# A gated delta-rule kernel on one core: inverses and their coupling moved into the tile of A, five k/q buffers, earlier loads for the next head's inverses

## The chip, the cores and the metric

The kernel runs on one core of one Trainium2 chip. The metric is device time in microseconds (us) for one execution of the whole program; the time of before is the median of 3 runs. Engines are named as the profile names them: PE (matmul), PEld (its weight loads), DVE, ACT, POOL and SP (which issues all DMAs of this kernel, in program order). PEq, SPq and so on are the sequencers.

## The reference

One layer with two parallel branches over 2048 tokens of width 1024, fed by one input projection to 7 x 1024 columns. Group A is a gated MLP with spatial mixing over blocks of 128 tokens. Group B, which the change is about, is a gated DeltaNet with 8 heads of width 128, in chunks of 64 tokens:

```
A  = strict_lower((k*beta) @ k.T * L)            # 64 x 64, L = decay between positions
T  = inverse(I + A)                              # triangular
u  = T @ (v*beta);  w = T @ (k*beta*exp(decay))
v_new = u - w @ state
o     = (q*exp(decay)) @ state + (q @ k.T * L) @ v_new
state = state*exp(decay_last) + (k*exp(decay_last - decay)).T @ v_new
```

Then a normalisation and a gate for the branch, the output projection, a gated per-layer embedding and a last normalisation. The state runs through all 32 chunks of a head, so those steps follow one another; everything else is a large projection.

## The kernel before, in words

The tokens go in two passes of 1024, and in each pass the 8 heads follow one another. In a pass PE first computes the v columns of group A (`v_unit`), then for each head three units of projections: `kq_unit` (k and q), `vu_unit` (v of group B, u of group A) and `zz_unit` (two gates). A unit is 2 column blocks x 2 token blocks (b = 0, 1) of 512 tokens, 24 products `pj` each, in three-product float32r splits (high and low parts). The weights of a unit come by four DMAs (`raw`, L251) and are split by ACT and DVE into `whi` and `wlo`. After the heads follow `out_stream` (`pso`) and `gate_stream` (`pe`, `pg`).

Beside this stream runs the work of group B, for each head in four stages. Two chunks (128 tokens, index u of 4, in each b) share one 128 x 128 tile:

- `front` (L719): transposes k, forms `pkq` = k'[k q] on PE, and from it the tiles `AT` (A, transposed and scaled) and `QK`; the two diagonal 64 x 64 blocks of each AT go to DRAM (`atd`, L780).
- `inverse` (L811): POOL solves the 16 systems of a head at once by 63 steps of two tensor_tensor each (L179: multiply to `xtmp`, subtract from `xs`). The systems come back from DRAM in eight pieces `ain` (L822, two buffers), the unit matrix in `xs` (L815). The inverses are stored to `td` (L841) and loaded into the two diagonal blocks of the one tile `Dt` (L848), but only after the outputs of the head before are finished (`done`, L844).
- `chain` (L851): for each of 8 tiles u in turn seven float32 products of 128 columns: k with the state (`pc<-S,kq`), Dt with r (`pc<-r,Dt`, in the very first tile of a head of the first pass `pc<-vn,Dt`), q with the state (`po<-S,kq`), AT with the first half of that result (`pc<-x,AT`), Dt with the corrected r, then kd with w (the new state) and QK with w (the output).
- `finish` (L919): normalises, transposes and gates the output and stores it (`done`).

The order of every engine's instructions is fixed when the program is built. The class `Flow` (L31) plays a clock: `mm` advances it on PE, `fl.op` books the other engines (`gtt`, L178, books a POOL tensor_tensor at 330 + 1.6 ns for each element), tasks sleep until a given time (`yield fl.t + 4500`), and `drive` and `step` put a task's instructions into PE's stream of projections when the clock says that its data are there. What the clock says is not what the chip does: on the chip each engine goes through its list in order and waits at semaphores. So an instruction whose data come later than the clock said holds up all that stands behind it on its engine. `take`, `give` and `free` with the table CAPS (L103) keep count of buffers: four `kq` tiles are two heads.

Of the kernel before, what the change touches and what calls it, by code (L numbers as in the profile page):

```python
# [18 lines left out]
ALU = mybir.AluOpType  # L19
# [83 lines left out]
CAPS = {"pj": 2, "tr": 2, "m": 2, "kq": 4, "pre": 2, "acc": 3, "uz": 3, "ot": 1, "gn": 2, "R": 2, "raw": 4, "w": 5}  # L103
# [3 lines left out]
def trunk(tc, a, out):  # L107
# [78 lines left out]
    with ExitStack() as outer:  # L186
# [18 lines left out]
        bsd = [dp.tile([P, P], F32, name=f"bsd{i}") for i in range(NH)]  # L205
        hsc = [dp.tile([P, D], F32, name=f"hsc{i}") for i in range(NT)]
# [82 lines left out]
        def x_load(row0, halves=False):  # L289
            xs = []  # L290
            for i in range(4):
# [5 lines left out]
                else:  # L297
                    xt = [gt("kq", "xt", [P, D], 4)]
# [54 lines left out]
        def inv_rms(xs):  # L353

            dg = gt("xs", "dg", [P, 4, P], 1)
# [16 lines left out]
        def prep_store(p):  # L372
            for b in range(2):
# [5 lines left out]
                for i in range(4):  # L379
                    xs.append([gt("kq", "xt", [P, D], 4)])  # L380
                    dma(xs[i][0], a["x"][row0 + i * P:row0 + (i + 1) * P, :])
                    yield fl.t + 1500
# [47 lines left out]
        def scalars(ab):  # L430
            beta = gt("beta", "beta", [P, 64], 2)
            act(beta, ab[:, 8:16].rearrange("p f t -> p (f t)"), AF.Sigmoid)
            yield fl.t + 3500
            yield from fl.take("gn")
# [27 lines left out]
            pc = bank("tr", "pcs", [P, 3, 64])  # L462
            for i, m in enumerate((uincl, mgt, ones)):
                g0 = mm(pc[:, i, :], m, g, True, True)
            ex = gt("ex", "ex", [P, 3, 64], 2)
# [173 lines left out]
        def zz_unit(X, p, ui, h, st, norms, mids):  # L639
# [14 lines left out]
            for b in range(2):  # L654
                yield lambda: len(done) >= st["i"] + b - 3
                ps = yield from proj(X, ui, 0, b)
                fl.spawn(z_silu(ps, st), 170, 1)
                if b == 0:
                    next_w(ui + 1, 0)
            if mids:  # L660
                banks = yield from proj_both(X, ui, 1, mids)
            for b in range(2):
                ps = banks[b] if mids else (yield from proj(X, ui, 1, b, rest_w(ui + 1) if b else None))
                fl.spawn(z_post(ps, st["U"], b, gz), 170, 1)
            fl.spawn(mix(p, h, gz, ws, bs, gns, norms), 1500, 2)

        def kq_unit(X, p, ui, h, st):
# [3 lines left out]
            for b in range(2):  # L671
                yield fl.free("kq")
                fl.used["kq"] = fl.used.get("kq", 0) + 1
                kq = gt("kq", "kq", [P, 4, 2, P], 4)
# [44 lines left out]
        def front(p, h, b, st):  # L719
            beta, gh, gl, ex, ne = SC[p]  # L720
            cs = slice(h * 8 + b * 4, h * 8 + b * 4 + 4)
            while len(done) < st["i"] + b - 3 or len(fronts) < st["i"] + b:
# [7 lines left out]
            qe = gt("qe", "qe", [P, 4], 4)  # L730
# [14 lines left out]
            tt(bn, bn, beta[:, cs], ALU.mult)  # L745
            st["iv"][b] = power(iv, iv, phalf[:, :4], after=f)
            AT = gt("AT", "AT", [P, 4, P], 4)
            QK = gt("QK", "QK", [P, 4, P], 4)
            for u2 in range(2):
# [24 lines left out]
                fl.give("m")  # L774
            yield f
# [7 lines left out]
            st["B"].append((kq, kd, vn, AT, QK, bn, qe))  # L783
# [27 lines left out]
        def inverse(p, h, st):  # L811
            while 2 * len(inverted) < st["i"]:
                yield fl.t + 300
            xs = gt("xs", "xs", [P, 8, 64], 1)
            dma(xs, a["xinit"])  # L815
            tmp = gt("xtmp", "xtmp", [P, 160], 1)
# [23 lines left out]
            td = dp.tile([64, 16, 64], F32, tag="td", bufs=2, name="td")  # L840
            dma(td.rearrange("(k c) s i -> (c s) k i", c=8), xs)  # L841
            inverted.append(1)
            yield fl.t + 2600
            while len(done) < st["i"]:  # L844
                yield fl.t + 300
# [536 lines left out]
```

## Time and profile before

| | |
|---|---|
| median of 3 runs | 2336.96 us (2334.66 to 2454.31) |
| the profiled execution | 2334.43 us, span 2332.7 us from the first to the last instruction |
| granted PE clock, mean over the span | 0.985 of full speed |
| busy: PE, PEld, DVE, ACT, POOL | 96%, 81%, 55%, 43%, 49% of the span |

The stages can be read from the timeline by tile names: the first pass's heads run from about 125 to 907 us, those of the second from about 996 to 1720 us, then the output projection to 2085 us and the gate to the end. A granted clock of 1.00 is 2.4 GHz, 0.50 is 1.2 GHz. Busy times of PE are modelled ends of a pipeline; the distance between the starts of two products tells what one costs in a dense stretch.

### The profile page before, as it was taken

To read this page: it belongs to the slowest core of one execution; us is meant where nothing else is said; L and a number is where in the kernel's file an instruction comes from. 1 tells how busy PE (TensorE), PEld (TensorE's weight loads), DVE (VectorE), ACT (ScalarE), POOL (GpSimd) and SP (SyncE) were. 2 spreads that over 40 slices of the span, in tenths; PEclk is the share of its full clock that TensorE was granted. 3 is DMA by queue.
4 is the path that set the end of the run, shared out by engine and by line. 5 is a ranking of instruction groups with operands and counts; after the bars stand their busy time and mean duration, and the time that the engine had idled before them with its cause. 6 is when DMAs were issued, how large, how long until landed. Compare 5 with 4: busy or idle time off the path is not lost.

```text
span 2332.7 us, 34766 instructions
## 1 busy us (share of the span) xinstructions
PE 2250.4 (96%) x11884; PEld 1878.9 (81%) x11884; DVE 1293.3 (55%) x2845; ACT 999.1 (43%) x2398; POOL 1131.6 (49%) x2246
## 2 busy tenths in 40 slices
PE   8999899999999999999899999999989999999998
PEld 8988688787787779987788878778778878878886
DVE  5465375574665755347466566575664243346665
ACT  5554354453444443445345454454432232244443
POOL 1118668586686772137768668668660000001111
PEclk9999999999999999999999999999999999999999
DMA  5632232323222243222332332232453466452221
GB/s 185 228 117 88 73 99 79 98 72 101 89 87 80 79 148 114 77 76 80 89 98 80 96 99 78 87 87 85 126 167 121 150 200 194 139 185 74 79 77 63
DMA packets 249201, 253.22 MB, mean 109 GB/s; under 512 B 66112, under 2 KB 163904, under 8 KB 249024
## 3 DMA queue, kind: packets, MB, share of 16 engines
q1 hardware_dynamic: 249024, 251.01, 34.6%
q8 instruction: 93, 1.52, 0.3%
q14 instruction: 84, 0.69, 0.1%
HBM read 195.89 MB, written 55.05 MB: 108 GB/s over the span
## 4 chain that ended last, share of the span: by engine, by line
PE 78%; POOL 11%; DMA 5%; issue 2%; DVE 2%; ACT 1%; SPq 1%; POOLq 0%; DVEq 0%; ACTq 0%
PE pj L121 36%; PE pso L121 13%; PE pg L121 7%; PE pc L121 6%; PE pv L121 6%; POOL xs L179 5%; POOL xtmp L179 4%; DMA Dt<-td 2%; PE po L121 2%; PE pe L121 2%; PE pkq L121 1%; DMA wo<-in_wo 1%; DMA td<-xs 1%; PE pm L121 1%; PE ph L127 1%
## 5 line engine op out<-in xcount | busy, mean ns | idle before, releaser
L179 POOL TENSOR_TENSOR xtmp<-ain,xs 128x132 f32<-128x132 f32 (+47 forms) x1008 | 462.4, 459 | 250.9 <-DMA ain<-atd 180.4
L179 POOL TENSOR_TENSOR xs<-xs,xtmp 128x132 f32<-128x132 f32 (+47 forms) x1008 | 483.2, 479 | 79.0
L175 POOL TENSOR_TENSOR rstd<-rstd,nhalf 128x1 f32<-128x1 f32 x64 | 45.8, 722 | 577.3 <-DVE rstd L159 290.3
L121 PE MATMUL pj<-xlo,whi 128*128 128x512 f32 x768 | 315.3, 411 | 0.0
L121 PE MATMUL pj<-xhi,wlo 128*128 128x512 f32 x768 | 314.9, 410 | 0.0
L121 PE MATMUL pj<-xhi,whi 128*128 128x512 f32 x768 | 314.2, 409 | 0.0
L121 PE MATMUL pj<-xrhi,whi 128*128 128x512 f32 x768 | 313.2, 408 | 0.0
L121 PE MATMUL pj<-xrhi,wlo 128*128 128x512 f32 x768 | 312.3, 407 | 0.0
L121 PE MATMUL pj<-xrlo,whi 128*128 128x512 f32 x768 | 311.0, 405 | 0.0
L152 DVE SCALAR_TENSOR_TENSOR acc<-pre,cw,acc 128x512 f32<-128x512 f32 x288 | 227.8, 791 | 23.9 <-ACT acc L135 19.4
L121 PE MATMUL pso<-wolo,yhi 128*128 128x512 f32 x512 | 204.9, 400 | 2.3 <-DVE wolo L148 2.2
L121 PE MATMUL pso<-wohi,ylo 128*128 128x512 f32 x512 | 205.3, 401 | 0.0
L121 PE MATMUL pso<-wohi,yhi 128*128 128x512 f32 x512 | 202.5, 395 | 0.0
L148 DVE TENSOR_TENSOR wlo<-raw,whi 128x512 fp32r<-128x512 f32 x224 | 163.9, 734 | 62.5 <-ACT whi L135 61.6
L135 ACT ACTIVATE whi<-raw 128x512 fp32r<-128x512 f32 x224 | 140.3, 629 | 95.2 <-PE pj L121 71.0
L135 ACT ACTIVATE yhi<-yraw 128x512 fp32r<-128x512 f32 x128 | 80.3, 630 | 215.3 <-PE pso L121 208.6
L121 PEld LDWEIGHTS pj<-xlo,whi 128*128 128x128 f32 x768 | 147.2, 192 | 24.3
L121 PEld LDWEIGHTS pj<-xhi,wlo 128*128 128x128 f32 x768 | 147.0, 191 | 23.9
L121 PEld LDWEIGHTS pj<-xhi,whi 128*128 128x128 f32 x768 | 146.9, 191 | 23.7
L121 PEld LDWEIGHTS pj<-xrhi,wlo 128*128 128x128 f32 x768 | 145.7, 190 | 25.1
L121 PEld LDWEIGHTS pj<-xrlo,whi 128*128 128x128 f32 x768 | 146.0, 190 | 24.5
L148 DVE TENSOR_TENSOR ylo<-yraw,yhi 128x512 fp32r<-128x512 f32 x128 | 89.5, 701 | 135.9 <-ACT yhi L135 133.2
(202 smaller groups left out, 4858.3 us busy)
## 6 DMA issues: line engine op xcount, KB each, us to landing
raw<-in_wu SPq DMA_DIRECT2D x224, 256.0 KB
ain<-atd SPq DMA_DIRECT2D x128, 256.0 KB
yraw<-ysc SPq DMA_DIRECT2D x128, 256.0 KB
vsc<-gv SPq DMA_DIRECT2D x64, 128.0 KB
gn<-vsc SPq DMA_DIRECT2D x32, 256.0 KB
ysc<-gn SPq DMA_DIRECT2D x32, 256.0 KB
ysc<-zb SPq DMA_DIRECT2D x32, 256.0 KB
wo<-in_wo SPq DMA_DIRECT2D x32, 256.0 KB
```

The source lines that it names most:

```text
L121: nc.tensor.matmul(o, lhsT, rhs, start=start, stop=stop)
L127: nc.tensor.transpose(o, i, ident)
L135: nc.scalar.activation(o, i, func, **kw)
L148: nc.vector.tensor_tensor(o, x, y, op)
L152: nc.vector.scalar_tensor_tensor(o, x, sc, y, op0, op1)
L175: nc.gpsimd.tensor_tensor(o, x, y, ALU.pow)
L179: nc.gpsimd.tensor_tensor(o, x, y, op)
```

## The change

The inverses no longer go to a tile of their own. They are loaded into the diagonal blocks of the tile `AT` itself, from which A's diagonal has been stored before. The lower left block of that tile holds the coupling of the two chunks (rescaled by ACT with a new decay factor `ex[:, 3]`), and a new task `join` computes the block above the diagonal: the coupling already multiplied by an inverse, four products of 64 columns for each b (`pgt`) and one DVE multiplication. A tile u of the chain is then six products instead of seven, four of which depend on one another (k with the state, M with r0, M with r, kd with w). Also changed: the inverses may be loaded before the head before is finished; the next head's unit matrix (`xs`, now two buffers) and first piece `ain` are loaded when 56 of the 63 steps are done (`solved`), and the POOL loop follows 1000 ns on the planner's clock after the loads instead of 4500; `front` waits for the chain two heads back (`chained`), not for its finished output; `kq` has five buffers; `gtt` is booked at 375 + 1.95 ns; the two halves of `zz_unit` are exchanged; the state between the passes is kept in DRAM (`ssc`) and loaded at the head of the chain (`S0`); two masks come in one late load. The diff, cut to its core:

```
-CAPS = {... "kq": 4, ...}
+CAPS = {... "kq": 5, ...}
 def gtt(o, x, y, op, after=None):
-        return fl.op("pool", 330 + 1.6 * width(o), after)
+        return fl.op("pool", 375 + 1.95 * width(o), after)
 def front(p, h, b, st):
-            while len(done) < st["i"] + b - 3 or len(fronts) < st["i"] + b:
+            while len(chained) < st["i"] + b - 3 or len(fronts) < st["i"] + b:
...
+            tt(fb, bn, ex[:, 3, cs], ALU.mult)
...
-                    stt(AT[:, u], pkq[:, j, 0], bn[:, u:u + 1], L[:, u], ALU.mult, ALU.mult)
+                    f = stt(AT[:, u], pkq[:, j, 0], bn[:, u:u + 1], L[:, u], ALU.mult, ALU.mult)
+                    act(AT[64:128, u, 0:64], pkq[64:128, j, 0, 0:64], AF.Copy, after=f,
+                        scale=ex[64:128, 3, h * 8 + b * 4 + u:h * 8 + b * 4 + u + 1])
...
+            nc.vector.memset(AT[0:64, :, 64:128], 0.0)
 def inverse(p, h, st):
+            while 2 * len(solved) < st["i"]:
+                yield fl.t + 300
+            xs = gt("xs", "xs", [P, 8, 64], 2)
+            dma(xs, a["xinit"])
             load(0)
+            while 2 * len(inverted) < st["i"]:
+                yield fl.t + 300
             load(1)
-            yield fl.t + 4500
+            yield fl.t + (1000 if h else 4500)
...
-                if jj == 7 and jc < 6:
+                if jj == 7:
                     yield f
-                    load(jc + 2)
+                    if jc < 6:
+                        load(jc + 2)
+                    else:
+                        solved.append(1)
...
             yield fl.t + 2600
-            while len(done) < st["i"]:
-                yield fl.t + 300
-            for d in range(2):
-                dd = slice(d * 64, d * 64 + 64)
-                dma(Dt[dd, :, dd], td.rearrange("c (u d) i -> d c u i", d=2)[d])
-            fl.spawn(chain(p, h, st), 4500, 0)
+            for b in range(2):
+                for d in range(2):
+                    dd = slice(d * 64, d * 64 + 64)
+                    dma(st["B"][b][3][dd, :, dd], td[:, b, :, d])
+            fl.spawn(join(0, st), 5000, 0)
+            fl.spawn(join(1, st), 5600, 1)
+            fl.spawn(chain(p, h, st), 5000, 0)
+def join(b, st):
+            M, fb = st["B"][b][3], st["B"][b][6]
+            yield from fl.take("tr")
+            pg = bank("tr", "pgt", [P, 4, 64])
+            for u in range(4):
+                f = mm(pg[:, u], M[:, u], M[:, u, 64:128], True, True)
+            yield f
+            f = tt(M[0:64, :, 64:128], pg[0:64], fb[0:64, :, None].to_broadcast([64, 4, 64]), ALU.mult)
+            fl.give("tr")
+            yield f
+            st["G"].append(b)
 def chain(p, h, st):
-            while len(done) < st["i"] or len(st["R"]) < 2:
+            while len(chained) < st["i"] or len(st["R"]) < 2:
                 yield fl.t + 300
-            Sp = state[:, h, :]
+            if p:
+                Sp = gt("S0", "S0", [P, P], 1)
+                dma(Sp, ssc[h])
...
-                        yield stt(r, pc[:, 0], ne[:, cu], vn[:, u], ALU.mult, ALU.add)
-                    f = mm(pc[:, 1], Dt[:, b * 4 + u], r, True, True)
+                        f = stt(r0[lo], pc[lo, 0], ne[lo, cu], vn[lo, u], ALU.mult, ALU.add)
+                        stt(r[up], pc[up, 0], ne[up, cu], vn[up, u], ALU.mult, ALU.add)
+                    yield f
+                    f = mm(pc[:, 1], M[:, u], r0, True, True)
...
-                    yield act(x1[0:64], pc[0:64, 1], AF.Copy)
-                    f = mm(pc[:, 2], AT[:, u], x1, True, True)
+                    f = act(r[lo], pc[lo, 1], AF.Copy, scale=-1.0)
+                    act(w[lo], pc[lo, 1], AF.Copy, scale=bn[lo, uu])
+                    yield f
+                    f = mm(pc[:, 2], M[:, u], r, True, True)
...
-                    yield tt(r[64:128], r[64:128], pc[64:128, 2], ALU.subtract)
-                    yield mm(pc[:, 1], Dt[:, b * 4 + u], r, True, True)
-                    yield ts(w, pc[:, 1], bn[:, u:u + 1], None, ALU.mult)
+                    yield ts(w[up], pc[up, 2], bn[up, uu], None, ALU.mult)
...
+                        if last:
+                            dma(ssc[h], Sn)
...
+                chained.append(1)
```

How this moves instructions is read from the order of the built programs. On PE, at the start of the chain of head 2 of the first pass, this stands in before (`pkq` is the front of head 3, `pj` the projections, `pq` transposes of q):

```order
L121 MATMUL pkq<-kqlo,kqhi 128x256
L121 MATMUL pkq<-kqhi,kqlo 128x256
L121 MATMUL pj<-xhi,whi 128x512
L121 MATMUL pc<-vn,Dt 128x128
L121 MATMUL pj<-xlo,whi 128x512
L121 MATMUL pj<-xhi,wlo 128x512
L121 MATMUL pj<-xhi,whi 128x512
L121 MATMUL pc<-x_218,AT 128x128
L121 MATMUL pj<-xlo,whi 128x512
```

And this in the changed kernel, at the start of the same chain:

```order
L121 MATMUL pj<-xhi,wlo 128x512
L121 MATMUL pj<-xhi,whi 128x512
L121 MATMUL pgt<-AT 128x64 x8
L121 MATMUL pc<-r_220,AT 128x128
L121 MATMUL pj<-xlo,whi 128x512
L121 MATMUL pj<-xhi,wlo 128x512
L121 MATMUL pj<-xhi,whi 128x512
L121 MATMUL pc<-r,AT 128x128
L121 MATMUL pj<-xlo,whi 128x512
```

The front of head 3 is gone from there: its last `pkq` stood one `pj` ahead of the chain and now stands 70 `pj` ahead of it. Head 2's own last `pkq` lies 288 `pj` ahead of its chain in before, and 349 now. Eight joins stand at the chain's start.

On SP, around the store (`td`) and the load (`Dt`) of head 1's inverses in the first pass, before (`atd` is head 2's front, `ain` its systems; `ws`, `bs`, `raw` and `gn` are loads for the projection units and the mixing):

```order
L780 DMA atd_3726<-AT_3566 64x4x64 x2
L841 DMA td_3758<-xs_2883 128x8x64
L848 DMA Dt_217<-td_3758 64x8x64 x2
L780 DMA atd_3726<-AT_3785 64x4x64 x2
L815 DMA xs_3901<-in_xinit 128x512
L822 DMA ain_3904<-atd_3726 128x1x512
L822 DMA ain_3906<-atd_3726 128x1x512
L642 DMA ws_4012<-in_ws 128x128
L645 DMA bs_4015<-in_bs 128x128
L251 DMA raw_4017<-in_wu 128x512
```

The same place in the changed kernel, where the inverses are loaded into the tiles AT:

```order
L831 DMA ain_3953<-atd_3735 128x1x512
L649 DMA ws_4004<-in_ws 128x128
L652 DMA bs_4007<-in_bs 128x128
L252 DMA raw_4009<-in_wu 128x512
L252 DMA raw_4011<-in_wu 128x512
L252 DMA raw_4013<-in_wu 128x512
L252 DMA raw_4015<-in_wu 128x512
L659 DMA gn_4017<-vsc0_73 128x4x128
L659 DMA gn_4019<-vsc0_73 128x4x128
L860 DMA td_4029<-xs_2931 128x8x64
L831 DMA ain_4031<-atd_3735 128x1x512
L866 DMA AT_2588<-td_4029 64x4x64 x2
```

The first piece of the next head's systems is loaded ahead of the store of the inverses, and eight loads of the projections and the mixing now stand between the two; in before these stood behind the load of the inverses.

On SP in the second pass, in the changed kernel, the load of the state `S0` for head 6's chain stands behind loads of the output stage (`wo`, `yraw`) and of the mixing (`gn`):

```order
L1012 DMA wo_18504<-in_wo 128x512
L1059 DMA yraw_18507<-ysc0_75 128x4x128
L1059 DMA yraw_18509<-ysc0_75 128x4x128
L1059 DMA yraw_18511<-ysc0_75 128x4x128
L1059 DMA yraw_18513<-ysc0_75 128x4x128
L659 DMA gn_18518<-vsc1_74 128x4x128
L659 DMA gn_18520<-vsc1_74 128x4x128
L1059 DMA yraw_18529<-ysc0_75 128x4x128
L891 DMA S0_18558<-ssc6_93 128x128
L831 DMA ain_18574<-atd_18209 128x1x512
```

In before the state of a head stayed in SBUF, and no such load stood there.

## Rows read from the trace of the kernel before

**Rows 1.** The page's part 1: busy time and share of the span, instructions of each engine.

```profile
PE 2250.4 (96%) x11884; PEld 1878.9 (81%) x11884; DVE 1293.3 (55%) x2845; ACT 999.1 (43%) x2398; POOL 1131.6 (49%) x2246
```

**Rows 2.** Who PE waited for, whole span: in total, times, longest.

```profile
PE pc L121 <- DMA Dt<-td: 53.7, 15, 9.5
```

**Rows 3.** PE's timeline, first pass: start, us, what [idle before <-releaser].

```profile
338.79 0.28 PE L121 MATMUL pkq<-kqhi,kqlo 128*128 128x256 f32 x1
340.35 0.46 PE L121 MATMUL pc<-vn,Dt 128*128 128x128 f32 x2 [1.28 <-DMA Dt<-td]
...
422.39 0.40 PE L121 MATMUL pj<-xhi,wlo 128*128 128x512 f32 x1
422.62 0.39 PE L121 MATMUL pj<-xhi,whi 128*128 128x512 f32 x1
...
428.64 0.40 PE L121 MATMUL pj<-xhi,whi 128*128 128x512 f32 x1
434.15 0.77 PE L121 MATMUL pc<-vn,Dt 128*128 128x128 f32 x2 [5.12 <-DMA Dt<-td]
...
435.15 0.63 PE L121 MATMUL pj<-xhi,wlo 128*128 128x512 f32 x1
435.57 0.63 PE L121 MATMUL pj<-xhi,whi 128*128 128x512 f32 x1
```

**Rows 4.** Stretches of PE: length, busy (instructions), granted clock, DMA share, GB/s.

```profile
240.00:910.00 670.00, 631.72 (x3403) 0.97 0.31 93
1090.00:1760.00 670.00, 645.31 (x3388) 0.98 0.33 98
434.00:436.00 2.00, 1.85 (x5) 0.50 0.61 149
438.00:440.00 2.00, 2.00 (x8) 0.56 0.73 220
```

**Rows 5.** Timeline of POOL, with one row of DVE (351.78), first pass.

```profile
333.36 0.54 POOL L179 TENSOR_TENSOR xs<-xs,xtmp 128x8 f32<-128x8 f32 x1
347.05 0.29 POOL L179 TENSOR_TENSOR xtmp<-ain,xs 128x63 f32<-128x63 f32 x1 [11.74 <-DMA ain<-atd]
...
351.53 0.29 POOL L179 TENSOR_TENSOR xs<-xs,xtmp 128x58 f32<-128x58 f32 x1
351.78 0.69 DVE L148 TENSOR_TENSOR wlo<-raw,whi 128x512 fp32r<-128x512 f32 x1
351.90 0.72 POOL L179 TENSOR_TENSOR xtmp<-ain,xs 128x57 f32<-128x57 f32 x1
...
427.42 0.21 POOL L179 TENSOR_TENSOR xs<-xs,xtmp 128x8 f32<-128x8 f32 x1
439.33 0.29 POOL L179 TENSOR_TENSOR xtmp<-ain,xs 128x63 f32<-128x63 f32 x1 [10.74 <-DMA ain<-atd]
...
526.15 0.68 POOL L179 TENSOR_TENSOR xs<-xs,xtmp 128x8 f32<-128x8 f32 x1
```

**Rows 6.** SP's timeline, both passes: start and us of the issues, what they load.

```profile
427.66 0.38 SPq L841 DMA_DIRECT2D td<-xs  x1
430.55 1.22 SPq L848 DMA_DIRECT2D Dt<-td  x2
...
1657.95 11.13 SPq L1014 DMA_DIRECT2D yraw<-ysc  x4
...
1671.78 0.36 SPq L1014 DMA_DIRECT2D yraw<-ysc  x1
```

**Rows 7.** PE's timeline: neighbouring float32 products of 64 and of 128 columns.

```profile
93.12 0.39 PE L121 MATMUL pcs<-g,mgt 128*128 128x64 f32 x2
93.35 0.39 PE L121 MATMUL pcs<-g,ones 128*128 128x64 f32 x2
...
344.57 0.38 PE L121 MATMUL pc<-w,kd 128*128 128x128 f32 x2
344.79 0.39 PE L121 MATMUL po<-w,QK 128*128 128x128 f32 x2
```

More of the change, by code (lines that the diff above doesn't have):

```diff
@@ L100, in drain @@
             self.idle()
-CAPS = {"pj": 2, "tr": 2, "m": 2, "kq": 4, "pre": 2, "acc": 3, "uz": 3, "ot": 1, "gn": 2, "R": 2, "raw": 4, "w": 5}
+CAPS = {"pj": 2, "tr": 2, "m": 2, "kq": 5, "pre": 2, "acc": 3, "uz": 3, "ot": 1, "gn": 2, "R": 2, "raw": 4, "w": 5}
 TABLES = {AF.Exp: 1, AF.Sigmoid: 2, AF.Silu: 3, AF.Gelu_apprx_tanh: 4}
@@ L205, in trunk @@
         bsd = [dp.tile([P, P], F32, name=f"bsd{i}") for i in range(NH)]
+        ssc = [dp.tile([P, P], F32, name=f"ssc{i}") for i in range(NH)]
         hsc = [dp.tile([P, D], F32, name=f"hsc{i}") for i in range(NT)]
@@ L353, in inv_rms @@
         def inv_rms(xs):
-            dg = gt("xs", "dg", [P, 4, P], 1)
+            dg = gt("xs", "dg", [P, 4, P], 2)
             for i, (xt,) in enumerate(xs):
@@ L433, in scalars @@
             yield fl.t + 3500
+            yield from fl.take("pre")
+            mk = gt("pre", "mk", [P, 3, P], 2)
+            dma(mk, a["masks"])
             yield from fl.take("gn")
@@ L461, in scalars @@
             fl.give("tr")
-            pc = bank("tr", "pcs", [P, 3, 64])
-            for i, m in enumerate((uincl, mgt, ones)):
+            pc = bank("tr", "pcs", [P, 4, 64])
+            for i, m in enumerate((mk[:, 0], mk[:, 1], ones, mk[:, 2])):
                 g0 = mm(pc[:, i, :], m, g, True, True)
-            ex = gt("ex", "ex", [P, 3, 64], 2)
+            if not SC:
+                act(mgt_r, mk[:, 1], AF.Copy)
+            fl.give("pre")
+            ex = gt("ex", "ex", [P, 4, 64], 2)
             g0 = act(ex, pc, AF.Exp, after=g0)
@@ L729, in front @@
             iv = gt("iv", "iv", [P, 4], 4)
-            qe = gt("qe", "qe", [P, 4], 4)
+            fb = gt("fb", "fb", [P, 4], 4)
+            qe = gt("qe", "qe", [P, 4], 6)
             kd = gt("kd", "kd", [P, 4, P], 4)
@@ L774, in front @@
                 fl.give("m")
+            nc.vector.memset(AT[0:64, :, 64:128], 0.0)
+            fl.op("dve", 330)
             yield f
@@ L835, in inverse @@
                 f = gtt(xs[:, :kk, j + 1:], xs[:, :kk, j + 1:], t_, ALU.subtract)
-                if jj == 7 and jc < 6:
+                if jj == 7:
                     yield f
-                    load(jc + 2)
+                    if jc < 6:
+                        load(jc + 2)
+                    else:
+                        solved.append(1)
             yield f
-            td = dp.tile([64, 16, 64], F32, tag="td", bufs=2, name="td")
-            dma(td.rearrange("(k c) s i -> (c s) k i", c=8), xs)
+            td = dp.tile([64, 2, 4, 2, 64], F32, tag="td", bufs=2, name="td")
@@ L894, in chain @@
                     outs.append(0)
-                    fl.spawn(gather(ot[:, u], po[:, 1], sso[:, u:u + 1], first, outs), fo - fl.t, 0)
+                    fl.spawn(gather(ot[:, u], po[:, 1], sso[:, uu], first, outs), fo - fl.t, 0)
                     if more:
                         yield f
-                        Sn = state[:, h, :] if last else gt("S", "S", [P, P], 2)
+                        Sn = gt("S", "S", [P, P], 2)
                         if first:
@@ L960, in stage @@
                 yield from fl.take("kq")
-                t = gt("kq", name, [P, 2, 512], 4)
+                t = gt("kq", name, [P, 2, 512], 5)
                 tiles = [t[:, 0], t[:, 1]]
@@ L1265, in stream @@
             yield from out_stream()
-        done, fronts, inverted, SC, mixed, stored, vdone, prepped, Ls = [[] for _ in range(9)]
+        done, chained, fronts, solved, inverted, SC, mixed, stored, vdone, prepped, Ls = [[] for _ in range(11)]
         xready = [0, 0]
@@ L1284, in trunk @@
         nc.vector.memset(carry, 0.0)
-        state = cp.tile([P, NH, P], F32, name="state")
         fetch(0)
@@ L1299, in trunk @@
         X0 = x_tiles()
-        Dt = gt("Dt", "Dt", [P, 8, P], 1)
-        x1 = gt("x1", "x1", [P, P], 1)
+        r0 = gt("r0", "r0", [P, P], 1)
         def setup():
-            nc.vector.memset(Dt.rearrange("p u i -> p (u i)"), 0.0)
-            nc.vector.memset(x1, 0.0)
-            fl.op("dve", 1400)
+            nc.vector.memset(r0, 0.0)
+            fl.op("dve", 200)
             act(nega, nega, AF.Exp)
             ts(nega, nega, -1.0, None, ALU.mult)
-            act(mgt_r, mgt, AF.Copy)
             yield
@@ L1361, in layout @@
         "ident": np.eye(P, dtype=np.float32),
-        "uincl": (r[:, None] <= r[None, :]).astype(np.float32),
-        "mgt": (r[:, None] > r[None, :]).astype(np.float32),
+        "masks": c(np.stack([r[:, None] <= r, r[:, None] > r,
+                             np.where(r < 64, (r[:, None] > r) & (r[:, None] < 64),
+                                      (r[:, None] <= r) & (r[:, None] > 63))], 1).astype(np.float32)),
         "xinit": (ii == pi // 16 + 8 * ki).astype(np.float32),
```

45 lines of the change are left out of this document (23 added, 22 removed).

## The prediction, made blind

> **What bounds the kernel now.** I read the page's busy shares first: PE is busy for 96% of the span, every other engine for about half of it or less [rows 1]. So only PE's idle time, its slow clock or its work can give anything back. Next I read whom PE waits for. One group stands out: the chain's first product waits for the load of the inverses 15 times, that is in 15 of the 16 heads, for 53.7 us in all and 9.5 at most [rows 2]. Then I followed one such wait, in head 2 of the first pass (heads count from 0), through the timelines of PE, POOL and SP. The front's last `pkq` ends at 339.07 [rows 3]. POOL's 63 steps begin at 347.05, 8.0 us later (store of A, loads back), and end at 427.63, after 80.6 us [rows 5]. The store is issued at 427.66 and the two loads from 430.55 [rows 6]; the product that needs them starts at 434.15 after a wait of 5.12 [rows 3], 6.5 us behind POOL's end. From `pkq` to product that is 95.1 us, in which PE had some 89 us of work (95.1 less the waits of 1.28 and 5.12). So PE hands over the front's products too late by the length of the wait. POOL meanwhile stands still between two loops from 333.90 to 347.05, 13.15 us, waiting for that same front [rows 5]: PE waits for POOL and POOL for PE, in a ring with one head of work in it.
>
> The wait has a second price. After it PE's granted clock is 0.50, and 0.56 four microseconds later [rows 4]; the projections stand 0.42 us apart, where before the wait it was 0.23 [rows 3]. Over about 6 us at nearly half speed a fall costs some 2.8 us of PE time.
>
> **The change part by part.** Durations come from the profiled execution: 2332.7 us of span and 1.7 around it, 2334.4 in all, 2.5 less than the median of the runs shown. The sum starts from 2334.4.
>
> *The waits.* In the new order the last `pkq` of head 2 stands 349 projections ahead of its own chain, where it stood 288. Counted instruction by instruction (0.23 us for a projection, 0.22 for a float32 product [rows 3, 7]), the PE work between a head's front and its chain rises from 88 to 94 us in heads 1 to 6 of both passes to 98 to 111. Needed are 8.0 + 80.6 + 6.5, as above, and 1.2 for two load issues more (the two of before take 1.22 [rows 6]): 96.3 us. The slack is 2 to 14 us, and the waits in those heads go. In the last head of a pass the work is 89.5 and 92.7 us; its loop runs without a neighbour's front and store and is shorter, so I leave it at most 2 us short. I take off all of the 53.7 and put what comes back under new lateness below.
>
> *The clock.* In the two stretches of heads, 670 us each, the granted clock is 0.97 and 0.98 [rows 4]: 0.03 x 670 + 0.02 x 670 = 33.5 us of full-speed time are lost at most. Part of the slow time is idle and counted already, up to 13.5 us (the 53.7, a quarter of it at half speed). Between 20 and 33 I take 20, the lower end, since short waits remain.
>
> *PE's work.* Of the seven products of a tile six remain: 128 tiles, 128 products of 0.22 us less [rows 7], 28.2 us. The joins add 128 products of 64 columns. The trace has no join, but it has float32 products of 64 columns, 0.23 us apart, beside products of 128 columns at 0.22 [rows 7]: 128 x 0.22 = 28.2 at one end, 29.4 at the other. With two products more by the order, the net is between 0 and +1.5; I take +0.4. If joins were to cost by their columns, half, the net would be 14 us less; that is the lower bound.
>
> The Trainium skill, TensorE: Matmul & The Clock Gate, section Back-to-back issue gap, gives the isolated gap as columns / 2.4 + 2.5 ns; by it a pass of 64 columns takes 29 ns, a join of two passes 58 ns and all joins 7.5 us (an estimate from that page), and the sum would be some 21 us lower. The same section says that in a real stream the weight load sets the spacing too, and the equal spacing of 64 and 128 columns here agrees with that [rows 7]; the measured spacing decides.
>
> *POOL.* The next head's first piece is loaded after 56 of 63 steps, so the 7 short steps that are left hide it; the next front stands 45 to 94 projections ahead of the chain now, in before 0 to 21. The 13.15 us between loops shrink to a few. This gives PE nothing directly; it gives the slack used above.
>
> *New lateness.* SP issues in program order. Behind the new place of the store come eight other loads (`ws`, `bs`, four `raw`, two `gn`) ahead of it in heads 0 and 1 of the first pass and 0 to 3 of the second, or ahead of the loads into AT in two heads more. The four `raw` loads wait for buffers that the splits give back late, about where the next `zz_unit` starts on PE. That point is 9.5 us ahead of the chain in the first pass's head 0, but shrinks to 0.7 by its last heads; in the second pass from 12.1 to 3.9. A wait on SP holds what is queued behind it: the store, the first `ain` of the next head, the loads into AT, and `S0`. For `S0` this is worst at the end: behind `yraw` loads in heads 6 and 7, and the fifth `yraw` of before stood 13.8 us behind the first, the four taking 11.13 to issue [rows 6]. The nearest row of what a late load costs PE is 3.6 us from issue to use (430.55 to 434.15 [rows 3, 6]). At the one end all lie within the slack, 0; at the other 11 heads pay 3.6 each, 40 us, and six falls of the clock at 2.8, 17 more, 56 in all. I take 1 us for each of heads 0 to 2 and 2 for head 7 of the first pass, 1 each for heads 3 to 5 of the second, 2.5 for head 6 and 4.5 for head 7: 15, and one fall of 2.8, about 18. That is nearer the lower end, as the slack covers most heads.
>
> *At nothing.* ACT's additional copies and scalings (ACT is 43% busy), DVE's memsets, the join's multiplication and the halves of the correction (55%) [rows 1], the exchange of the halves of `zz`, the fifth `kq`, the state through DRAM, the masks. The chain's four dependent products have projections between them, as the five had; no other wait of PE comes near the 53.7 us of the load. If that cover were gone, each tile would pay a few tenths of a microsecond, for 128 tiles some 30 us; this lies within the range.
>
> *Sum.* 2334.4 - 53.7 - 20 + 0.4 + 18 = 2279.
>
> **The rivals.**
>
> *Nothing is late next.* All loads arrive in the slack: 2334.4 - 53.7 - 20 + 0.4 = 2261. For it speaks the slack of 2 to 14 us; against it the eight loads ahead of the store, and `S0` behind `yraw`. With cheap joins as well it would be 2247.
>
> *SP is late everywhere.* The waits change their name only: inverses and states come behind loads that stall SP, 56 us in place of 18, 2317. For it speaks the order of SP, in which those eight loads stood behind the load of the inverses before; against it that PE reaches the `zz_unit`, which frees them, ahead of the chain in every head.
>
> *POOL is the pace, and slower.* If the ring is as long as POOL's loop and the gap behind it, nothing is gained by handing over fronts earlier: 80.6 + 13.15 = 93.75 us a head, 2334, the change not doing what it says. It turns into a loss when the loop stretches: POOL's steps are slowed by DVE's, and a step of 0.29 us takes 0.72 beside a DVE operation with two inputs in SBUF [rows 5]. The change adds work to DVE, and a loop that is never held up by the front runs all through the densest stretches. Head 3's loop took 87.5 us (439.33 to 526.83 [rows 5]); were all so, with the gap as it is, a head would take 100.65, 6.9 more for 14 intervals, 97 us, 2431. It decides from about 93.8 us of loop and gap upward. Against it: the gap falls, and the added DVE operations are small, some with PSUM inputs.
>
> The Trainium skill, GPSIMD Engine Reference, section Specifications, says that GpSimd shares its SBUF interfaces with VectorE and contends with DVE instructions that have two SBUF inputs; the stretched step agrees [rows 5].
>
> **How the numbers follow.** The forecast, 2279, has a chance of 0.50, with a range of its own from 2262 to 2297; nothing late 0.14; SP late everywhere 0.26; POOL as the pace 0.10, half of that at a loss. About 2% is what a measurement of this kernel can tell from no change: 2336.96 x 0.98 = 2290. Faster than that come all of the case with nothing late, four fifths of the forecast (0.40) and a sixth of SP's case (0.04): 0.58. Slower by 2% comes half of POOL's case, 0.05. The rest, 0.37, is within. The range runs from 2257 (nothing late and a part of the cheap joins) to 2330 (SP late with a lost cover of the chain), and leaves out about 2 in 10.
>
> **What would show it.** In the profile of the changed kernel PE's waits for the load of the inverses into AT should be gone or short in heads 1 to 6, with the granted clock of the two stretches near 0.99. POOL's gaps between loops should be a few microseconds, and its loops 75 to 88 us as now. The products of a join should stand 0.22 to 0.23 us apart; half of that would mean that they cost by their columns. PE's busy time should fall by the clock's share, about 20 us, its instructions hardly. New waits should be for the loads into AT or for `S0`, and on SP's queue for `raw` or `yraw` buffers; the last heads of the second pass should show the longest. The prediction is wrong if PE waits as long as before under another name, if POOL's loops grow past 94 us, or if PE waits in the chain for ACT or DVE, which I cost at nothing.

## The result, and the profile after

The changed kernel takes 2393.2 us (median of 4 runs, 2392.3 to 2394.4); before 2336.4 (4 runs). The ratio is 1.0246, 95% interval 1.0226 to 1.0266: it is slower, outside the forecast range on the far side. One run of before, 2454.3 us, fell in a slower state of the chip, and the ratio leaves it out. Before was measured again beside every later run, at medians of 2331.2 to 2333.9 us, and their ratios go by that; a difference to the changed kernel's 2393.2, which was measured once, is good to some 5 us.

The part of the page on busy shares, of the changed kernel, which answers to [rows 1]:

```profile
PE 2303.5 (96%) x11888; PEld 1878.2 (79%) x11888; DVE 1348.4 (56%) x2948; ACT 1072.2 (45%) x2655; POOL 1127.3 (47%) x2246
```

PE's busy time is up by 53 us at four instructions more. The modelled ends of neighbouring products cover small holds, which so count as busy. So the holds are sought in the weight loads' waits and in the distances between starts. Who waited for whom on PE (first three rows) and on PEld (last three), of the changed kernel; total, times, longest:

```profile
PE pc L121 <- DMA S<-ssc: 20.5, 4, 11.9
PE pgt L121 <- DMA AT<-td: 16.7, 9, 3.9
PE pkq L121 <- DVE kqlo L148: 7.5, 16, 0.8
...
PEld pc L121 <- DVE r L152: 47.6, 102, 1.0
PEld pc L121 <- ACT w L135: 42.9, 110, 0.6
...
PEld pkq L121 <- DVE kqlo L148: 17.2, 32, 1.1
```

The chain's groups of PEld in the kernel before, where `x` stood in the place of the `w` that ACT forms now:

```profile
PEld pc L121 <- DVE w L157: 18.2, 91, 0.6
PEld pc L121 <- ACT x L135: 16.4, 95, 0.7
PEld pc L121 <- DVE r L152: 12.1, 58, 0.9
```

The wait for the inverses [rows 2] fell from 53.7 us to 16.7, but the state's load costs 20.5, and the chain's weight loads wait 90.5 us for `r` and ACT's `w` instead of 28.5 for `r` and `x`. How that looks in one tile, from the timelines of PE, PEld, DVE and ACT (second pass; ahead of it the joins of head 0):

```profile
1137.83 1.00 PE L121 MATMUL pgt<-AT 128*128 128x64 f32 x8
1138.67 0.44 PE L121 MATMUL pc<-S,kq 128*128 128x128 f32 x2
...
1144.13 0.73 DVE L152 SCALAR_TENSOR_TENSOR r<-pc,ne,vn 64x128 f32<-64x128 f32 x2
...
1144.63 0.40 PE L121 MATMUL pj<-xrhi,whi 128*128 128x512 f32 x1
1144.92 0.30 PEld L121 LDWEIGHTS pc<-r,AT 128*128 128x128 f32 x2 [0.32 <-DVE r L152]
1144.92 0.49 PE L121 MATMUL pc<-r,AT 128*128 128x128 f32 x2
...
1145.24 0.39 PE L121 MATMUL po<-S,kq 128*128 128x128 f32 x2
...
1145.50 0.27 ACT L135 ACTIVATE r<-pc 64x128 f32<-64x128 f32 x1 [1.06 <-PE pc L121]
1145.68 0.35 ACT L135 ACTIVATE w<-pc,bn 64x128 f32<-64x128 f32 x1
...
1145.70 0.39 PE L121 MATMUL pj<-xrhi,wlo 128*128 128x512 f32 x1
1146.08 0.30 PEld L121 LDWEIGHTS pc<-r,AT 128*128 128x128 f32 x2 [0.42 <-ACT w L135]
1146.08 0.49 PE L121 MATMUL pc<-r,AT 128*128 128x128 f32 x2
...
1146.41 1.06 PE L121 MATMUL pm<-ws,gn 128*128 128x128 f32 x8
```

The product at 1144.92 stands 0.29 us behind a projection (0.23 is dense), that at 1146.08 0.38 behind one, and the products behind them 0.32 and 0.33 instead of 0.22. Each starts 0.05 us after the second half-tile operation ahead of it ends (1144.86 and 1146.03), though it needs only the first. The same holds in the whole trace: no weight load of M's first product starts before the second half of `r` ends (105 of 120 within 0.08 us after it), and none of its second product before `w` ends (113 of 128). The built program has these waits in 120 and 128 tiles: a product there waits until all earlier readers of the PSUM bank that it writes are done, and the second half is one of them:

```
PE  MATMUL pc<-r0,AT   waits for   DVE  SCALAR_TENSOR_TENSOR r<-pc,ne,vn   (r[up])
PE  MATMUL pc<-r,AT    waits for   ACT  ACTIVATE w<-pc,bn                  (w[lo])
```

Against [rows 5], POOL now goes from one loop to the next almost without a pause (346.35 to 346.94, was 13.15 us), but this loop takes 94.0 us (252.32 to 346.35), where head 2's took 80.6. In heads 1 to 6 of both passes the loops take 88 to 101 us, with gaps of 0.1 to 7.8 behind them; before, 77 to 88 with gaps of 11 to 16. POOL's busy time did not grow (1127.3 us, was 1131.6), so the loops are longer by waits:

```profile
252.32 0.29 POOL L179 TENSOR_TENSOR xtmp<-ain,xs 128x63 f32<-128x63 f32 x1
...
345.81 0.54 POOL L179 TENSOR_TENSOR xs<-xs,xtmp 128x8 f32<-128x8 f32 x1
346.94 0.29 POOL L179 TENSOR_TENSOR xtmp<-ain,xs 128x63 f32<-128x63 f32 x1 [0.59 <-DMA ain<-atd]
```

To see where the time came from, I took from the distance of each product's start to the one before what that one costs in a dense stretch (0.2305 us a projection, 0.111 a pass of a float32 product, 0.105 to 0.13 other forms). The rest is PE time lost ahead of the product, called idle by the profile or not. Sums in us, with three of the experiments below (the load of `Dt` by its listed waits):

| lost ahead of | before | changed | planner's clock waits for halves | other bank | other bank, front order, S0 early |
|---|---|---|---|---|---|
| load of the inverses | 53.7 | 22.1 | 21.1 | 13.5 | 13.0 |
| load of the state S0 | 0.1 | 21.7 | 6.4 | 19.6 | 3.3 |
| the chain's other products | 16.5 | 63.4 | 33.9 | 22.1 | 27.0 |
| the front's `pkq` | 1.0 | 16.4 | 12.3 | 16.6 | 2.8 |
| projections `pj`, `pso` (the clock too) | 29.3 | 32.0 | 29.0 | 28.4 | 25.7 |
| everything else | 4.8 | 9.8 | 18.3 | 10.9 | -0.2 |
| sum | 105.4 | 165.4 | 121.0 | 111.1 | 71.6 |
| span less the sum | 2227.3 | 2226.6 | 2225.2 | 2225.9 | 2225.1 |

PE's own work is the same everywhere within 2.2 us; the 59.3 us of span are 46.9 in the chain, 15.4 in the front, 21.6 for S0, 31.6 less for the inverses, 7.7 in the last two groups of losses and -0.7 of work.

### The profile page after: what moved, and what is told of

Read it like the earlier page. It is cut to its first block, busy times and chain, and to the rows that moved or that the text cites. A ratio compares the mean times of both kernels' runs of the same rounds, so it can differ in the third digit from the quotient of the medians.

```text
span 2392.0 us, 35273 instructions
## 1 busy us (share of the span) xinstructions
PE 2303.5 (96%) x11888; PEld 1878.2 (79%) x11888; DVE 1348.4 (56%) x2948; ACT 1072.2 (45%) x2655; POOL 1127.3 (47%) x2246
## 3 DMA queue, kind: packets, MB, share of 16 engines
q1 hardware_dynamic: 251840, 252.32, 34.3%
## 4 chain that ended last, share of the span: by engine, by line
PE 70%; DVE 9%; POOL 7%; DMA 6%; ACT 4%; issue 3%; SPq 1%; DVEq 0%; POOLq 0%; ACTq 0%
PE pj L121 27%; PE pso L121 13%; PE pv L121 7%; PE pg L121 7%; PE pc L121 6%; POOL xs L179 3%; POOL xtmp L179 3%; PE po L121 2%; DVE acc L152 2%; DVE r L152 2%; PE pe L121 2%; DMA td<-xs 1%; PE pgt L121 1%; DMA AT<-td 1%; PE pm L121 1%
## 5 line engine op out<-in xcount | busy, mean ns | idle before, releaser
L179 POOL TENSOR_TENSOR xtmp<-ain,xs 128x132 f32<-128x132 f32 (+47 forms) x1008 | 456.9, 453 | 149.3 <-DMA ain<-atd 73.4
L121 PEld LDWEIGHTS pj<-xrhi,whi 128*128 128x128 f32 x768 | 145.8, 190 | 25.6
```

The source lines that it names most:

```text
L121: nc.tensor.matmul(o, lhsT, rhs, start=start, stop=stop)
```

## The experiments

**The planner's clock waits for both halves.** Nothing but the point from which the planner lets the chain go on:

```
-  stt(r[up], pc[up, 0], ne[up, cu], vn[up, u], ALU.mult, ALU.add)
+  f = stt(r[up], pc[up, 0], ne[up, cu], vn[up, u], ALU.mult, ALU.add)
-  act(w[lo], pc[lo, 1], AF.Copy, scale=bn[lo, uu])
+  f = act(w[lo], pc[lo, 1], AF.Copy, scale=bn[lo, uu])
```

> The changed kernel with one thing altered: the planner's clock lets the chain go on only when the second of the two half-tile operations of a step is done (r[up] ahead of M with r0, w[lo] ahead of M with r). The operations and the semaphores stay; a projection more stands between the dependent products. Theory H (the second halves hold PE: the product waits for both, its weight load comes 0.2 to 0.5 us late, 240 times, 42 us ahead of M's products and 11 ahead of the q product behind them): these short holds fall to about a quarter, time about 2358 (2345 to 2370). Rival L (the loads into AT and of S0, 37 us of waits, set the time, and PE would have waited there for what the short holds take): no change, 2385 to 2397. Rival C (a product that depends on the one before costs more on PE by itself): no change.

Measured: 2348.8 us, 44 less than the changed kernel, ratio to before 1.0067 (1.0050 to 1.0084). The weight loads' waits for `r` and `w` fell to 17.8 and 15.2 us. The chain's steps are no shorter; PE merely has a projection more to do in the meantime. Of the 44 us, 30 are the chain's, 15 those of S0, which this edit doesn't touch; why S0 gained is not shown beyond the new order of instructions. Rivals L and C fall.

**One operation for r, and one for r and w.** The first run below puts one operation in place of two halves of `r`, with a product over 64 rows; the second does so for `w` too, with a product that writes 64 columns:

```
-  f = stt(r0[lo], pc[lo, 0], ...); stt(r[up], pc[up, 0], ...)
+  f = stt(r, pc[:, 0], ne[:, cu], vn[:, u], ALU.mult, ALU.add)
-  f = mm(pc[:, 1], M[:, u], r0, True, True)
+  f = mm(pc[:, 1], M[lo, u], r[lo], True, True)
...
-  f = mm(pc[:, 2], M[:, u], r, True, True)
+  f = mm(pc[up, 1], M[:, u, 64:128], r, True, True)
-  yield ts(w[up], pc[up, 2], bn[up, uu], None, ALU.mult)
+  yield ts(w, pc[:, 1], bn[:, uu], None, ALU.mult)
```

> The changed kernel with one operation for r in place of two halves: r is formed over all 128 partitions at once, and the product with r0 becomes one over the first 64 rows of M and r, so that no zero half is needed. The halves behind it (r[lo], w[lo]) stay. Theory H: the wait ahead of M's first product (47.6 us of weight loads waiting for DVE, 102 times) goes, that ahead of the second stays: about 25 us faster, 2368 (2360 to 2376). Rival L: 2385 to 2397. Rival C: no change, or a little, as 64 rows are no cheaper.

> As the run before, and the second product with M writes only its 64 columns of the second chunk, into the place below the first product's result, so that w is formed by one operation over all 128 partitions and ACT forms only r[lo] ahead of it. Every step has one operation now. Theory H: both groups of waits go (47.6 and 42.9 us of waiting weight loads fall to the 10 to 18 us that such groups have in the kernel before), 40 to 50 us faster, 2347 (2338 to 2358). Rival L: 2385 to 2397, with the waits for AT and S0 grown by what the chain gives back.

Measured: 2388.4 us (1.0231, 1.0210 to 1.0253) and 2395.4 (1.0261, 1.0240 to 1.0281); both missed. The waits for S0 had gone in both (3.2 and 3.4 us), and the waits for the second halves shrank, but the losses ahead of the q product rose from 10.7 to 24.1 and 23.2 us and those of `pj` from 24.5 to 37.4 and 51.6. The experiment had brought in a cost of its own. What the product over 64 rows adds to it, the next run measures; the product that writes 64 columns, in the second run only, was not tested by itself.

**64 rows alone.** The changed kernel with one product in another form:

```
-  f = mm(pc[:, 1], M[:, u], r0, True, True)
+  f = mm(pc[:, 1], M[lo, u], r0[lo], True, True)
```

> The changed kernel with one product in another form: M's first product contracts over the first 64 rows of M and r0 alone (the other 64 rows of r0 are zero, so the result is the same); order and waits stay. It tests why one operation for r did not pay in the earlier run. Theory K (a product of 64 rows between products of 128 has its weight load, and that of the product behind it, uncovered by the products in front: the spacing of the q product behind it was 0.41 instead of 0.22 us there): 128 times 0.2 to 0.35 us, 25 to 45 us slower than the changed kernel, 2425 (2415 to 2440). Rival (it was the order): within 6 us of 2393.

Measured: 2411.2 us (1.0347, 1.0324 to 1.0370), 18 more than the changed kernel, or 0.14 us for each of 128 products: below the forecast size, with its sign. A part of the 18 may be the granted clock, 0.983 in the profiled run against 0.988. From its timeline of PE:

```profile
1161.12 0.39 PE L121 MATMUL pj<-xrhi,wlo 128*128 128x512 f32 x1
1161.49 0.48 PE L121 MATMUL pc<-r,AT 64*128 64x128 f32 x2
1161.90 0.49 PE L121 MATMUL po<-S,kq 128*128 128x128 f32 x2
1162.15 0.48 PE L121 MATMUL pj<-xrhi,whi 128*128 128x512 f32 x1
```

The q product stands 0.41 us behind the one of 64 rows; with 128 rows it was 0.32 above. This doesn't hang on the clock: where it was full, the median is 0.415 us in 115 tiles here and 0.325 in 116 of the changed kernel. So the two runs before say nothing against theory H; the run with the other bank tests it without such products.

**The other bank.** M's first result goes to a third slot of `po`, and the q product stands behind M's second product:

```
-  f = mm(pc[:, 1], M[:, u], r0, True, True)
+  f = mm(po[:, 2], M[:, u], r0, True, True)
-  if not first:
-      mm(po[:, 0], kq[:, u, 1, :], Sp, True, True)
-  f = act(r[lo], pc[lo, 1], AF.Copy, scale=-1.0)
-  act(w[lo], pc[lo, 1], AF.Copy, scale=bn[lo, uu])
+  f = act(r[lo], po[lo, 2], AF.Copy, scale=-1.0)
+  act(w[lo], po[lo, 2], AF.Copy, scale=bn[lo, uu])
   f = mm(pc[:, 2], M[:, u], r, True, True)
   if not first:
+      mm(po[:, 0], kq[:, u, 1, :], Sp, True, True)
```

> The changed kernel with the result of M's first product in the bank of po instead of pc, and the q product behind M's second product. Both halves of each step are still computed, in the old order on their engines; but the first product waits for r0 alone and the second for the two halves of r, no longer for r[up] and w[lo], as these read a bank that the product doesn't write. Theory B (PE was held by halves that it doesn't need, through the shared bank; the runs before showed that the planner's clock alone gives 44 us back when it waits for them): the groups of weight loads waiting for r and w (90 us) fall to 35 or less, 30 to 45 us faster, 2355 (2345 to 2365). Rival P (what helped there was only the wider spacing of the dependent products, a projection more; at the old spacing the product is late whatever it waits for): at most 12 us faster, 2381 to 2393.

Measured: 2338.9 us, 54 less than the changed kernel, 1.0022 (1.0009 to 1.0036) of before. Its waits on PEld:

```profile
PEld pc L121 <- ACT r L135: 11.0, 68, 0.3
...
PEld po L121 <- DVE r L152: 9.8, 49, 0.5
```

21 us in place of 90, with the same operations and the planner's clock as it was. PE waits here for `r`, no longer for `w`: in the built program none of these products waits for a second half, and in the trace 97 of 120 first products load their weights before the second half of `r` ends, 111 of 128 second ones before `w` ends (none in the changed kernel). So the shared bank held them, and not the place of the q product, which moved too.

**Halves alone, in the kernel before.**

```
-  yield stt(r, pc[:, 0], ne[:, cu], vn[:, u], ALU.mult, ALU.add)
+  f = stt(r[0:64], pc[0:64, 0], ne[0:64, cu], vn[0:64, u], ALU.mult, ALU.add)
+  stt(r[64:128], pc[64:128, 0], ne[64:128, cu], vn[64:128, u], ALU.mult, ALU.add)
+  yield f
```

> The kernel before with one thing of the change put in: r is formed in two halves of 64 partitions, one behind the other, and the planner's clock goes on with the first. Theory H: Dt's product waits for both, 0.36 us more in 112 tiles, 40 us, of which one part is slack: 20 to 35 us slower than before, 2357 to 2372, with a group of some 40 us of weight loads waiting for r. Rival L: within 6 us of before, since the wait for Dt shrinks by what the chain loses.

Measured: 2356.1 us, 1.0096 of before (1.0081 to 1.0111), just below the range of theory H. Its rows:

```profile
PE pc L121 <- DMA Dt<-td: 43.2, 14, 9.4
...
PEld pc L121 <- DVE r L152: 49.7, 101, 2.1
```

The group for `r` is 38 us larger than before and the wait for `Dt` 10.5 smaller: PE that is held in the chain comes later to the next load, and part of the price is hidden there.

**S0 early.**

```
   load(1)
+  if p:
+      st["S0"] = gt("S0", "S0", [P, P], 2)
+      dma(st["S0"], ssc[h])
```

> The changed kernel with the load of the state S0 (second pass) issued with the loads ahead of POOL's loop, into one of two buffers, some 85 us before its use and ahead of the weights' and yraw loads on SP. Theory: PE's four waits for S0 (20.5 us, the longest 11.9) go and nothing of them comes back, as they stand in the last heads: about 2372 (2368 to 2380). Rival: they only stand where PE would have waited for the second load into AT anyway, and that wait grows: within 6 us of the changed kernel's 2393.

Measured: 2379.9 us (1.0204, 1.0189 to 1.0219), 13 less. The four waits are gone; 7.2 us came back once as a wait for `r`. Why the longest of them stood there, from SP's timeline of the changed kernel (first the loads into AT of head 2, then S0 of head 6, and the product on PE that needs it):

```profile
440.86 0.38 SPq L860 DMA_DIRECT2D td<-xs  x1
441.34 0.63 SPq L831 DMA_DIRECT2D ain<-atd  x1
442.06 0.41 SPq L649 DMA_DIRECT2D ws<-in_ws  x1
...
443.00 1.84 SPq L252 DMA_DIRECT2D raw<-in_wu  x4
444.90 2.84 SPq L659 DMA_DIRECT2D gn<-vsc  x2
447.78 2.60 SPq L866 DMA_DIRECT2D AT<-td  x4
...
1712.64 3.24 SPq L1059 DMA_DIRECT2D yraw<-ysc  x4
1715.94 3.02 SPq L659 DMA_DIRECT2D gn<-vsc  x2
1720.56 0.36 SPq L1059 DMA_DIRECT2D yraw<-ysc  x1
1720.96 0.51 SPq L891 DMA_DIRECT2D S<-ssc  x1
1724.60 0.80 PE L121 MATMUL pc<-S,kq 128*128 128x128 f32 x2 [11.93 <-DMA S<-ssc]
```

The loads into AT are issued 6.9 us behind the store, where before it was 2.9 [rows 6]. The fifth `yraw` waits 1.4 us until DVE has split an earlier one, and S0, which waits for nothing itself, is issued behind it at 1720.96; PE uses it at 1724.60 after a wait of 11.93.

**The front's order.** ACT scales the coupling behind DVE's three operations on `pkq`:

```
-  f = stt(AT[:, u], pkq[:, j, 0], ...); act(AT[64:128, u, 0:64], pkq[64:128, j, 0, 0:64], ...)
+  stt(AT[:, u], pkq[:, j, 0], ...)
   f = tt(QK[:, u2 * 2:u2 * 2 + 2], pkq[:, :, 1], ...)
+  for j in range(2):
+      act(AT[64:128, u, 0:64], pkq[64:128, j, 0, 0:64], ...)
```

> The changed kernel with ACT's two scalings of the coupling in the front moved behind DVE's three operations on the same bank pkq (before, DVE and ACT took turns on it, 0.38 to 0.42 us of waiting at each turn). Theory: DVE reaches the next split kqlo earlier, PE's waits for kqlo (7.5 us, 17.2 on the weight loads) fall to near those of before (0.4): 10 to 15 us faster, 2380 (2375 to 2385). Rival: kqlo is late because the fronts now stand where DVE has more to do, beside POOL's loop: no change, 2389 to 2396.

Measured: 2348.2 us (1.0058, 1.0038 to 1.0078), 45 less, three times the forecast. The turns, from the timeline of the changed kernel's DVE and ACT:

```profile
333.14 0.34 DVE L152 SCALAR_TENSOR_TENSOR AT<-pkq,bn,L 128x128 f32<-128x128 f32 x1
333.52 0.31 ACT L135 ACTIVATE AT<-pkq,ex 64x64 f32<-64x64 f32 x1 [1.00 <-DVE AT L152]
333.87 0.35 DVE L152 SCALAR_TENSOR_TENSOR AT<-pkq,bn,L 128x128 f32<-128x128 f32 x1 [0.38 <-ACT AT L135]
334.25 0.31 ACT L135 ACTIVATE AT<-pkq,ex 64x64 f32<-64x64 f32 x1 [0.42 <-DVE AT L152]
334.59 0.42 DVE L148 TENSOR_TENSOR QK<-pkq,L 128x256 f32<-128x256 f32 x1 [0.38 <-ACT AT L135]
```

PE's loss ahead of `pkq` fell from 16.4 to 2.5 us, as the theory says. The remainder was not foreseen: S0's loss fell by 16 us and that of the load into AT by 9, in an order of instructions that the planner laid out anew. How much of that is the earlier front, and how much the order, this run doesn't tell apart.

**The front's turns alone, in the kernel before.**

```
-  stt(AT[:, u], pkq[:, j, 0], bn[:, u:u + 1], L[:, u], ALU.mult, ALU.mult)
+  f = stt(AT[:, u], pkq[:, j, 0], bn[:, u:u + 1], L[:, u], ALU.mult, ALU.mult)
+  junk = gt("junk", "junk", [P, P], 2, BF16)
+  act(junk[64:128, 0:64], pkq[64:128, j, 0, 0:64], AF.Copy, after=f, scale=...)
```

> The kernel before with the front's turns alone put in: behind each of DVE's two operations that form AT, ACT scales a 64 x 64 corner of the same bank pkq into a scratch tile that nobody reads; the result is the same. Theory T (the turns themselves delay DVE and with it the split kqlo and the front; worth 13 us on PE's products in the changed kernel, and some 30 with what stands behind the front there): PE's waits for kqlo appear (some 12 to 16 us with the spacing), and the fronts' lateness adds to the waits for Dt: 13 to 30 us slower, 2350 (2344 to 2362). Rival S (it is the place of the fronts in the changed kernel, beside POOL's loop and away from the chain, that makes kqlo late; in before DVE has room): within 5 us of before.

Measured: 2329.4 us (0.9985, 0.9976 to 0.9994): no slower, as rival S had it, but not for its reason. Its waits on PE, DVE and PEld:

```profile
PE pc L121 <- DMA Dt<-td: 33.8, 10, 9.7
PE pkq L121 <- DVE kqlo L148: 4.4, 13, 0.7
...
DVE AT L152 <- ACT junk L135: 25.2, 60, 0.4
DVE QK L148 <- ACT junk L135: 24.0, 57, 2.7
...
PEld pkq L121 <- DVE kqlo L148: 14.4, 30, 1.0
```

DVE waits for ACT at each turn, though ACT writes a tile that nobody needs; what the two share is the bank that they read. The holds ahead of `pkq` appear here too, 14.2 us against 1.0; the loss ahead of the chain's products with `Dt` falls from 62.2 to 46.4 us. So it is the turns, not the place, that make `kqlo` late, and as these sums have it the kernel before hides them in a wait that the changed kernel has lost.

**POOL's in-order waits.** The changed kernel without the inverse root in `finish`:

```
-  yield power(sso, sso, nhalf[:, :4], after=f) + 1500
+  yield f + 1500
```

> The changed kernel without POOL's inverse root of the output's norm in finish (sso; 32 operations of 1.2 us): the outputs are left unnormalised there. These operations stand in POOL's list between the steps of the substitution and wait for the end of a chain, 130 us of waiting inside the heads' loops, where they waited 45 in the kernel before. Theory P (POOL, running without a gap, is the pace of the heads: its loops are 94 us, not 80, by these waits): the loops shrink to about 87, the waits for AT and a part of S0's go, 15 to 30 us faster, 2370 (2362 to 2378). Rival E (PE is the pace, POOL has slack; AT is late by SP's order): at most 8 us faster, 2385 to 2393, POOL's gaps grow by what the loops lose.

Measured: 2394.2 us (1.0277, 1.0256 to 1.0297), no gain; theory P falls. (The granted clock was 0.984 in the profiled run against 0.988, some 10 us at full speed, so a gain of that size could be hidden, which is less than the 15 to 30 of theory P.) Whom POOL waited for in the heads of the first pass, changed kernel:

```profile
POOL sso L175 <- DVE sso L152: 55.4, 9, 14.4
POOL L L183 <- ACT L L135: 40.4, 11, 5.2
POOL xtmp L179 <- DMA ain<-atd: 25.6, 7, 7.8
```

and without the root:

```profile
POOL L L183 <- ACT L L135: 73.7, 9, 12.4
POOL xtmp L179 <- DMA ain<-atd: 67.3, 10, 12.5
```

POOL's idle time only changes its name. So in the changed kernel the long loops are what POOL shows of a late PE, and not what holds PE up.

**Together.** The edit of the planner's clock, the front's order and S0:

> The three edits together: the planner's clock waits for both halves, S0 is loaded ahead of the loop, the coupling is scaled behind DVE's operations. If they add up: 2349 (the clock alone) less 4 (the waits for S0 left in that run) less 10 to 15 = about 2332 (2325 to 2340), level with before. If the fronts' waits are due to something else: about 2345.

Measured: 2312.9 us, 0.9916 (0.9901 to 0.9931): further than the first estimates add up to, and below their range. And the other bank in place of the edit of the planner's clock:

> The changed kernel with three edits: M's first result in the bank of po, the coupling scaled behind DVE's operations, S0 loaded ahead of the loop. Theory (three separate prices: the bank 54 us, the front's turns 13 on PE and more through an earlier POOL, S0 17 of waits in the run with the bank alone): 2339 less 13 to 30 for the front less about 15 for S0, 2303 (2294 to 2314), faster than before by over 1%. Rival (POOL is the pace by now, its loops of 84 to 90 us and the in-order waits in them set a head's time whatever PE holds): 2313 as in the run with the planner's clock, within 5.

Measured: 2298.7 us, 0.9863 (0.9841 to 0.9884), the fastest of all. From the run with the bank alone to this one S0's loss falls by 16.3 us, the front's by 13.8, and the rest by 9.4 (table); so the front's own price is some 14 us on PE, and what it gave more when undone alone were the waits of S0 and AT.

## Why the prediction was wrong

- *The step that failed is "at nothing".* It held that the chain's dependent products have projections between them "as the five had". They have, but two of the steps now hold two operations in sequence, 0.73 us of DVE and 0.27 and 0.35 of ACT in the tile above, and a product waits for the second through the bank. The prediction itself named waits of PE in the chain for ACT or DVE as a sign of being wrong. The price that I named for a lost cover, some 30 us, was 46.9. That no other wait came near the load's was read from PE's rows alone: the chain's weight loads already waited 46.7 us in the kernel before, in the three groups of PEld shown above (the table puts the loss there at 16.5). Two runs that leave the operations in place show it, by the planner's clock (44 us, of which 30 are the chain's) and by the bank (54, of which 41).
- *ACT's additional scalings in the front, also at nothing:* 15.4 us. ACT was idle enough; what cost PE time are the turns of DVE and ACT on one bank, 14 us when undone beside the other two edits. The share of busy time (43%) was the wrong place to read this from.
- *The waits, -53.7, and new lateness, +18:* the wait for the inverses went by two thirds, and S0 was worst behind `yraw` as foreseen, but with 11.9 us in head 6 where I took 2.5. New waits were 37.2 (16.7 + 20.5), within the bound of 56 and twice the value taken. The slack of 2 to 14 us was computed with a loop of 80.6; with loops of 88 to 101 there is none left in most heads.
- *The clock, -20:* the mean granted clock over the span went from 0.985 to 0.988. By the same working that is 0.015 x 2332.7 = 35.0 against 0.012 x 2392.0 = 28.7, or 6 us. In the first pass's stretch of heads the clock rose as forecast, from 0.97 to 0.99; in the second's it stayed at 0.98.
- *PE's work, +0.4:* right; span less losses is 0.7 us smaller. The joins ahead of the product at 1138.67 take 0.84 us for eight passes, 0.21 a join, as the measured rows had it [rows 7]. The isolated gap of the Trainium skill, TensorE: Matmul & The Clock Gate, section Back-to-back issue gap, from which the prediction estimated 0.058 us a join, does not describe them.
- *The rivals:* "SP is late everywhere" had the direction of one part. "POOL is the pace" got its loops past 93.8 us, but by in-order waits and not by slower steps (POOL is busy for 1127.3 us against 1131.6), and the run without the root shows that they do not set the time. Neither names what happened, and 0.05 on a loss was too little.
- *What was right:* with the prices of the bank, the front's turns and S0 undone, the kernel takes 2298.7 us against 2331.2 for before beside it: 32 us less, of the 55 forecast. So the waits for the inverses were worth going after; the sum failed by what the change brought in elsewhere.

## What to carry to other kernels

Count, for each step of a dependent chain, the operations up to the one that the product waits for in the built program, and not those that it needs. In these programs a product that writes into a PSUM bank waits for all earlier readers of that bank (54 us went with one result in another bank), and two engines that read one bank take turns (14 us). Where an edit is costed at nothing under a wait that the same change removes, its price has to come back into the sum; the same turns cost nothing before and 14 us after. A planner that believes in the shorter step puts the product too early; telling it the truth gave 44 us back here, and another bank for the result 54.

## What was not expected of the hardware

A float32 product of 64 rows between products of 128 costs more, not less: the run made for it was 18 us slower over 128 products (a part of that perhaps by the clock), with the product behind it 0.41 us away. A late product also pushes the one behind it, 0.32 and 0.33 us in the tile above where 0.22 is dense: its own two passes start 0.21 us apart (1144.92 and 1145.13), where 0.11 is dense. And an operation over 64 partitions takes as long as one over 128: the two halves of `r` take 0.73 us together, and the kernel before forms the whole `r` in 0.35 (median of 120).
